# Two rules of a hand-kept instruction order: the second sublayer is left as the table has it, and the later ones move their casts out of both token halves' norms

## The chip, the cores and the metric

The kernel runs on one core of one Trainium2 chip. The metric is device time in microseconds (us) of that core, as the median of several executions. TensorE (PE) does the matrix products and the transposes, VectorE (DVE) and ScalarE (ACT) the elementwise work, GpSimd (POOL) a few small powers and fills, and SyncE (SP) issues all loads and stores. Each engine works through its own list of instructions in the order in which the program puts them there.

## The reference

Two layers, each of three sublayers, six in all: a SwiGLU network, a token mixer and another SwiGLU network. The mixer of the first layer is an indexer-selected sparse attention ("dsa"), that of the second a differential attention ("diff"). Everything is float32: 256 tokens, width 1024, inner width 2752.

```python
for i in range(DEPTH):                       # DEPTH = 2
    mod = cond @ ada_w[i] + ada_b[i]
    sh0, sc0, g0, sh1, sc1, g1, sh2, sc2, g2 = jnp.split(mod, N_MOD, axis=-1)
    h = modulate(rmsnorm(x, pre_norm[i, 0]), sh0, sc0)
    y = swiglu(h, ffn_w_gate[i, 0], ffn_w_up[i, 0], ffn_w_down[i, 0])
    x = x + FFN_HALF * g0[:, None, :] * rmsnorm(y, post_norm[i, 0])
    h = modulate(rmsnorm(x, pre_norm[i, 1]), sh1, sc1)
    y = dsa_mixer(...) if i % 2 == 0 else diff_mixer(...)
    x = x + g1[:, None, :] * rmsnorm(y, post_norm[i, 1])
    h = modulate(rmsnorm(x, pre_norm[i, 2]), sh2, sc2)
    y = swiglu(h, ffn_w_gate[i, 1], ffn_w_up[i, 1], ffn_w_down[i, 1])
    x = x + FFN_HALF * g2[:, None, :] * rmsnorm(y, post_norm[i, 2])
```

## The kernel before

**Two token halves.** The 256 tokens are two halves of 128, t = 0 and t = 1, that go through the six sublayers (n = 0 to 5) one behind the other. In the second FFN part both share a product (`mm_joint`); elsewhere each half has its own matmuls, and the half t = 1 uses a weight block a few blocks after t = 0 did.

**Weights.** Every weight block of 128 rows is loaded in float32 into `raw` (5 buffers), and becomes two tiles: `hi`, a rounded copy, by a CAST on ACT, and `lo`, the rest, by a subtraction on DVE. Each product is three matmuls, activation hi by weight hi, hi by lo, and lo by hi. The pair normally is `whl` (7 buffers in a ring, each free again when t = 1 has used the block). `opens()` marks the first three blocks of a sublayer as early: their pair (`whi`, `wlo`) lies in the pool `big` (11 buffers) instead.

**From one sublayer to the next.** When the last matmul of a half's output is done (`ydown`, `ydsa`, `ydiff`), a chain of small steps leads to the next sublayer's first matmul. The letters are the labels that `link` gives the steps:

- a: ACT squares the two halves of the columns (`junk,ssy`), adds them up (`ssy`, then `rstdy`); POOL takes the power (`rstdy`).
- u: DVE multiplies the output by the gate (`u`); x: DVE adds it to the stream (`x0`, `x1`).
- b: ACT squares and sums the new x (`junk,ss`, `rstd`); POOL takes the power.
- h, r: DVE scales (`h<-x,g`) and modulates (`h<-h,rstd,sh`); t: PE transposes eight blocks (`ps_x`).
- c: ACT casts them to `HT` hi, DVE subtracts to `HT` lo. Then PE starts with `projA` (n = 1), `gate` (n = 2, 3, 5) or `projK` (n = 4).

The vectors `sh`, `g` and `pg` of the modulation are made between all this: POOL clears the tile, DVE accumulates (`sh<-araw`), PE spreads the sum over the partitions (`ps_m`), and ACT or DVE writes the result (`g<-ps_m`).

**What sets the order.** `ORDER`, a table of numbers, gives each engine's whole order; `arranged` then changes it around each sublayer's start, and `keep_order` makes it binding. Before, `arranged` goes over n = 1 to 5. On ACT and DVE it puts the early conversions ahead of the chain of t = 0, and holds weight casts back (`free`) so that only as many as `ROOM` allows stand behind a step a, b, x or r of t = 0. On PE it puts the transposes of t = 0 in among the last matmuls of t = 1's output:

```python
turns = [name for _, p, name in chain if p == "t"]
...
last = order.index(mark["out"][1, n - 1])
order[last - 4:last] = turns[:4] + order[last - 4:last] + turns[4:]
```

All instructions pass through one helper, so the profile gives them all the line L1027; they are told apart by their tiles.

Of the kernel before, what the change touches and what calls it, by code (L numbers as in the profile page):

```python
# [50 lines left out]
def trunk(ctx, tc, x, c, positions, ada_w, ada_b, pre_norm, post_norm, ffn_w_gate, ffn_w_up,  # L51
          ffn_w_down, dsa_w_in, dsa_w_out, diff_w_in, diff_w_out, diff_lambda, diff_subln, out):
    calls = []
    nc = Calls(tc.nc, calls)
# [272 lines left out]
    def ada_items(n, part):  # L327


        l, s = divmod(n, 3)  # L330
# [826 lines left out]
ROOM = {"a": 1, "b": 2, "x": 1, "r": 1}  # L1157


def arranged(orders, mark):  # L1160


    for n in range(1, 6):
        chain = mark["chain"][0, n]
        free = mark["free"] | {name for _, _, name in mark["chain"][1, n]}
        for order in (orders["EngineType.Activation"], orders["EngineType.DVE"]):
            part = {name: p for _, p, name in chain}
            at = [i for i, name in enumerate(order) if name in part]
            left = {p: sum(part.get(name) == p for name in order) for p in set(part.values())}
            new, held, room = [], [], 0  # L1170
            behind = at[-1] + 1
            ahead = [name for name in order[at[0]:behind + 12] if name in mark["early"]]
            for name in ahead:
                order.remove(name)
# [1 line left out]
            at = [i for i, name in enumerate(order) if name in part]
            for name in order[at[0]:at[-1] + 1]:
                if name in free:
                    held.append(name)
                else:  # L1180
                    new.append(name)
                    p = part.get(name)
                    if p:
                        left[p] -= 1
                        room = 0 if left[p] else ROOM.get(p, 0)
                new += held[:room]
                room, held = room - len(held[:room]), held[room:]
            order[at[0]:at[-1] + 1] = new + held
# [30 lines left out]
```

## Time and profile before

| | |
|---|---|
| time before, median of 3 runs | 1061.79 us (1056.61 to 1065.71) |
| the profiled execution's own time | 1061.59 us |
| its span, first to last instruction | 1059.8 us |
| around the span | 1.8 us |
| mean granted TensorE clock | 0.991 |
| busy: PE, DVE, ACT | 1017.6 us, 788.7 us, 522.6 us |

In a timeline a row is one instruction or several equal ones in a run: start in us from the span's start, length in us, engine, line, operation, output<-inputs, shape, count, and in brackets how long the engine stood idle before it and what ended that. PE's matmuls overlap, so a row of many is read by its length over its count. The granted clock is 1.0 at TensorE's 2.4 GHz and 0.5 at 1.2 GHz.

### The profile page before, as it was taken

The numbers are of one execution on the slowest core, as the hardware profiler recorded it, in microseconds if no ns is written. First come the engines' busy times: TensorE is split into PE (matmuls) and PEld (weight loads), VectorE is DVE, ScalarE is ACT, GpSimd is POOL, SyncE is SP. The second block draws the span as 40 slices with busy tenths as digits, with TensorE's granted clock in tenths as the row PEclk, the third lists the DMA queues.
The fourth block names the chain that finished last, engine by engine and source line by source line (L and its number), as shares of the span: only waits on it lengthen the run. The fifth ranks groups of instructions, "written<-read, shape, count | busy, mean of one in ns | idle before, by whom it ended". The sixth has DMA issues, their size and how long they took to land.

```text
span 1059.8 us, 15297 instructions
## 1 busy us (share of the span) xinstructions
PE 1017.6 (96%) x5936; PEld 876.0 (83%) x5936; DVE 788.7 (74%) x1121; ACT 522.6 (49%) x834; POOL 34.9 (3%) x49
## 2 busy tenths in 40 slices
PE   5999999988999999999999999999899899999997
PEld 2679997768777789998888999978777678999875
DVE  4769898887986978876688977857988675765643
ACT  3354434354475744453364544436467665544432
POOL 1000000001000200000010000000100100000000
PEclk9999999998999999999999999999999999999999
DMA  9949889983534477988757879866662533778531
GB/s 309 345 136 316 328 308 375 345 281 140 211 120 150 166 249 261 348 277 300 270 195 267 281 240 334 320 256 221 242 231 85 186 118 122 249 229 266 180 119 40
DMA packets 93732, 249.48 MB, mean 235 GB/s; under 512 B 6084, under 2 KB 24652, under 8 KB 93660
## 3 DMA queue, kind: packets, MB, share of 16 engines
q1 hardware_dynamic: 93660, 248.52, 67.9%
q8 instruction: 46, 0.75, 0.3%
q14 instruction: 26, 0.21, 0.1%
HBM read 247.44 MB, written 1.05 MB: 234 GB/s over the span
## 4 chain that ended last, share of the span: by engine, by line
PE 57%; issue 20%; DVE 5%; ACT 3%; POOL 1%; DMA 0%; DVEq 0%; POOLq 0%; ACTq 0%
PE ydown L1027 15%; PE up L1027 12%; PE gate L1027 11%; PE projQd L1027 2%; PE projQ L1027 2%; PE projA L1027 2%; PE projV L1027 2%; PE projK L1027 2%; PE ydiff L1027 1%; PE dsaS L1027 1%; PE ydsa L1027 1%; PE ps_m L1027 1%; PE diffS L1027 1%; PE dsaO L1027 1%; DVE whl L1027 1%
## 5 line engine op out<-in xcount | busy, mean ns | idle before, releaser
L1027 DVE TENSOR_TENSOR whl<-raw,whl 128x1024 fp32r<-128x1024 f32 (+3 forms) x201 | 228.7, 1151 | 94.9 <-ACT whl L1027 94.0
L1027 ACT CAST whl<-raw 128x1024 fp32r<-128x1024 f32 (+3 forms) x201 | 196.4, 996 | 172.4 <-PE ydown L1027 88.5
L1027 PE MATMUL gate<-HT,wj 128*128 128x256 f32 x1344 | 166.2, 284 | 1.3 <-DVE wj L1027 1.2
L1027 ACT CAST wj<-raw 128x1024 fp32r<-128x1024 f32 x112 | 116.3, 1048 | 103.6 <-PE up L1027 29.0
L1027 PEld LDWEIGHTS gate<-HT,wj 128*128 128x128 f32 x1344 | 163.4, 192 | 2.0 <-DVE wj L1027 1.7
L1027 PE MATMUL up<-HT,wj 128*128 128x256 f32 x1344 | 164.4, 283 | 0.1
L1027 DVE TENSOR_TENSOR wj<-raw,wj 128x1024 fp32r<-128x1024 f32 x112 | 134.8, 1221 | 39.5 <-ACT wj L1027 39.2
L1027 PEld LDWEIGHTS up<-HT,wj 128*128 128x128 f32 x1344 | 162.8, 192 | 0.6 <-ACT wj L1027 0.3
L1027 PE MATMUL ydown<-whl,ffj 128*128 128x512 f32 x672 | 159.3, 393 | 2.3 <-DVE whl L1027 2.3
L1027 PEld LDWEIGHTS ydown<-whl,ffj 128*128 128x128 f32 x672 | 126.0, 189 | 30.4 <-DVE whl L1027 3.1
L1027 PE MATMUL ydown<-whl,ffa 128*128 128x512 f32 (+1 forms) x368 | 90.9, 398 | 1.9 <-ACT whl L1027 1.9
L1027 PEld LDWEIGHTS ydown<-whl,ffa 128*128 128x128 f32 (+1 forms) x368 | 69.0, 191 | 20.2 <-issue 3.6
L1027 PE MATMUL gate<-whl,HT 128*128 128x480 f32 x276 | 71.3, 394 | 0.8 <-DVE whl L1027 0.7
L1027 DVE SCALAR_TENSOR_TENSOR pg<-araw,scond,pg 128x1024 f32<-128x1024 f32 x48 | 61.4, 1280 | 8.2 <-DMA araw<-in_ada_w_dram 7.7
L1027 PE MATMUL up<-whl,HT 128*128 128x480 f32 x288 | 66.0, 381 | 0.0
L1027 PEld LDWEIGHTS gate<-whl,HT 128*128 128x128 f32 x276 | 52.3, 192 | 13.1 <-issue 1.9
L1027 PEld LDWEIGHTS up<-whl,HT 128*128 128x128 f32 x288 | 53.5, 188 | 8.3 <-ACT sg L1027 0.5
L1027 DVE SCALAR_TENSOR_TENSOR g<-araw,scond,g 128x1024 f32<-128x1024 f32 x40 | 51.2, 1280 | 5.4 <-DMA araw<-in_ada_w_dram 4.9
L1027 DVE SCALAR_TENSOR_TENSOR sh<-araw,scond,sh 128x1024 f32<-128x1024 f32 x40 | 51.1, 1278 | 5.3 <-DMA araw<-in_ada_w_dram 5.0
L1027 POOL TENSOR_TENSOR rstdy<-rstdy,mhalf 128x1 f32<-128x1 f32 x12 | 6.6, 549 | 834.2 <-ACT rstdy L1027 834.2
L1027 PE MATMUL projV<-whl,HT 128*128 128x512 f32 x96 | 28.4, 416 | 0.0
L1027 ACT ACTIVATE junk<-x 128x512 f32<-128x512 f32 (+1 forms) x24 | 15.2, 632 | 26.3 <-DVE x L1027 15.2
(223 smaller groups left out, 1179.6 us busy)
## 6 DMA issues: line engine op xcount, KB each, us to landing
araw<-in_ada_w_dram SPq DMA_DIRECT2D x64, 1024.0 KB
raw<-in_ffn_w_down_dram SPq DMA_DIRECT2D x40, 1024.0 KB
raw<-in_ffn_w_gate_dram SPq DMA_DIRECT2D x56, 512.0 KB
raw<-in_ffn_w_up_dram SPq DMA_DIRECT2D x56, 512.0 KB
raw<-in_ffn_w_gate_dram SPq DMA_DIRECT2D x16, 960.0 KB
raw<-in_diff_w_in_dram SPq DMA_DIRECT2D x12, 1024.0 KB
raw<-in_ffn_w_up_dram SPq DMA_DIRECT2D x12, 960.0 KB
fraw<-in_ada_w_dram SPq DMA_DIRECT2D x32, 256.0 KB
```

Of the source, the lines that this page charges most:

```text
L1027: ins = method(*args, **kwargs)
```

## The change

Three things. `opens()` is no longer called ahead of `dsa_w_in`, so the first three blocks of the second sublayer (n = 1) are ordinary `whl` blocks. `arranged` starts at n = 2, so at n = 1 all engines follow the table as it stands. At n = 2 to 5 the holding back of casts (now `tidied`) is done for the chain of t = 1 too, and the writes of `ps_m` that are marked `spread` are put behind the last step b or x of t = 1.

```diff
     add_ffn(0, 0)
-    opens()
     add_matrix(dsa_w_in[0], D, 1024, 712)
...
+def tidied(order, chain, free):
+    part = {name: p for _, p, name in chain}
+    at = [i for i, name in enumerate(order) if name in part]
+    left = {p: sum(part.get(name) == p for name in order) for p in set(part.values())}
+    new, held, room = [], [], 0
+    for name in order[at[0]:at[-1] + 1]:
+        if name in free:
+            held.append(name)
+        else:
+            new.append(name)
+            p = part.get(name)
+            if p:
+                left[p] -= 1
+                room = 0 if left[p] else ROOM.get(p, 0)
+        new += held[:room]
+        room, held = room - len(held[:room]), held[room:]
+    return order[:at[0]] + new + held + order[at[-1] + 1:]
+
 def arranged(orders, mark):
-    for n in range(1, 6):
-        chain = mark["chain"][0, n]
-        free = mark["free"] | {name for _, _, name in mark["chain"][1, n]}
...
+    for n in range(2, 6):
+        chains = [mark["chain"][t, n] for t in range(2)]
+        own = [{name for _, _, name in chain} for chain in chains]
+        for e in ("EngineType.Activation", "EngineType.DVE"):
...
+            ahead = [name for name in order[at[0]:at[-1] + 13] if name in mark["early"]]
+            behind = [name for name in order[at[0]:end] if name in mark["spread"]]
+            order = [name for name in order if name not in set(ahead + behind)]
             order[at[0]:at[0]] = ahead
...
+            order = tidied(order, chains[0], mark["free"] | own[1])
+            order = tidied(order, chains[1], mark["free"])
+            place = max(order.index(name) for _, p, name in chains[1] if p in "bx" and name in order) + 1
+            order[place:place] = behind
```

**The start of the second sublayer (n = 1) on ACT.** `ssy_2009`, `rstdy_2010` and `x0` belong to t = 0; `ydown_1578` is the output of t = 1, and `ssy_2147` (now `ssy_2144`) its sum. Before:

```order
L1027 ACTIVATE rstdy_2010<-ssy_2009 128x1
L1027 CAST whl_2113<-raw_2107 128x712
L1027 ACTIVATE junk_2025,ss_2023<-x0_79 128x512
L1027 ACTIVATE junk_2027,ss_2023<-x0_79 128x513
L1027 ACTIVATE rstd_2024<-ss_2023 128x1
L1027 CAST whl_2192<-raw_2190 128x712
L1027 ACTIVATE junk_2150,ssy_2147<-ydown_1578 128x512
L1027 CAST HT_76<-ps_x_2034 128x512
L1027 CAST HT_76<-ps_x_2044 128x512
L1027 ACTIVATE junk_2153,ssy_2147<-ydown_1578 128x512
```

And now:

```order
L1031 CAST whl_2110<-raw_2105 128x712
L1031 ACTIVATE rstdy_2010<-ssy_2009 128x1
L1031 ACTIVATE junk_2025,ss_2023<-x0_79 128x512
L1031 ACTIVATE junk_2027,ss_2023<-x0_79 128x513
L1031 CAST whl_2189<-raw_2187 128x712
L1031 ACTIVATE rstd_2024<-ss_2023 128x1
L1031 ACTIVATE junk_2147,ssy_2144<-ydown_1578 128x512
L1031 ACTIVATE junk_2150,ssy_2144<-ydown_1578 128x512
L1031 ACTIVATE ssy_2144<-ssy_2144,epsc_83 128x1
L1031 CAST whl_2192<-raw_2187 128x712
L1031 CAST HT_76<-ps_x_2034 128x512
L1031 CAST HT_76<-ps_x_2044 128x512
```

Two casts moved in ahead of `rstdy` and `rstd` of t = 0, and the squares of t = 1 stand ahead of both casts to `HT` and no longer around them. Ahead of these rows both orders have three casts of 712 columns in the same place, to `whi` before and to `whl` now, then the two squares and the sum `ssy` of t = 0.

**The same start on PE.** `ps_x_2034` and `ps_x_2044` are the transposes of t = 0, `projA_2054` its first product. Before:

```order
L1027 MATMUL ydown_1578<-whl_1991,ffj_1575 128x512 x6
L1027 MATMUL ydown_1578<-whl_1994,ffj_1575 128x512
L1027 MATMUL ps_x_2034<-ident_87,h_2031 128x128 x4
L1027 MATMUL ydown_1578<-whl_1994,ffj_1575 128x512 x4
L1027 MATMUL ps_x_2044<-ident_87,h_2041 128x128 x4
L1027 MATMUL ydown_1578<-whl_1994,ffj_1575 128x512
L1027 MATMUL projA_2054<-whi_2063,HT_76 128x384
```

And now:

```order
L1031 MATMUL ydown_1578<-whl_1991,ffj_1575 128x512 x6
L1031 MATMUL ydown_1578<-whl_1994,ffj_1575 128x512 x6
L1031 MATMUL ps_x_2034<-ident_87,h_2031 128x128 x4
L1031 MATMUL ps_x_2044<-ident_87,h_2041 128x128 x4
L1031 MATMUL projA_2054<-whl_2063,HT_76 128x384
```

The last five matmuls of t = 1's output now stand ahead of the transposes of t = 0 and no longer among and behind them.

**The same start on DVE.** `u_2149` (now `u_2146`) is the output of t = 1 times its gate, `x1` its stream. Before:

```order
L1027 SCALAR_TENSOR_TENSOR h_2041<-h_2041,rstd_2024,sh_1400 128x512
L1027 TENSOR_TENSOR u_2149<-ydown_1578,pg_817 128x512
L1027 TENSOR_TENSOR HT_76<-ps_x_2034,HT_76 128x512
L1027 TENSOR_TENSOR HT_76<-ps_x_2044,HT_76 128x512
L1027 TENSOR_TENSOR u_2149<-ydown_1578,pg_817 128x512
L1027 SCALAR_TENSOR_TENSOR x1_81<-u_2149,rstdy_2148,x1_81 128x512 x2
```

And now:

```order
L1031 SCALAR_TENSOR_TENSOR h_2041<-h_2041,rstd_2024,sh_1400 128x512
L1031 TENSOR_TENSOR u_2146<-ydown_1578,pg_817 128x512 x2
L1031 TENSOR_TENSOR HT_76<-ps_x_2034,HT_76 128x512
L1031 TENSOR_TENSOR HT_76<-ps_x_2044,HT_76 128x512
L1031 SCALAR_TENSOR_TENSOR x1_81<-u_2146,rstdy_2145,x1_81 128x512 x2
```

The second `u` moved ahead of the two subtractions to `HT` lo.

**The start of the fourth sublayer (n = 3) on ACT, t = 1.** Before:

```order
L1027 ACTIVATE ssy_4932<-ssy_4932,epsc_83 128x1
L1027 ACTIVATE junk_4938,ssy_4932<-ydown_4455 128x512
L1027 CAST whl_5013<-raw_5011 128x960
L1027 ACTIVATE rstdy_4933<-ssy_4932 128x1
L1027 ACTIVATE junk_4948,ss_4946<-x1_81 128x512
```

And now:

```order
L1031 ACTIVATE ssy_4929<-ssy_4929,epsc_83 128x1
L1031 ACTIVATE junk_4935,ssy_4929<-ydown_4452 128x512
L1031 ACTIVATE rstdy_4930<-ssy_4929 128x1
L1031 CAST whl_5010<-raw_5008 128x960
L1031 ACTIVATE junk_4945,ss_4943<-x1_81 128x512
```

One cast moved from ahead of `rstdy` of t = 1 to behind it. The same single step is taken at n = 2, 4 and 5. Besides, at n = 4 the second of two `g<-ps_m` on DVE moved from behind the steps h and r of t = 1 to ahead of them. POOL's and SP's orders are the same before and after, and so is PE's order from n = 2 on.

## Rows read from the trace of the kernel before

**Rows 1.** The page's part 2, whole program: PE's granted clock in 40 slices of 26.5 us, in tenths of full speed.

```profile
PEclk9999999998999999999999999999999999999999
```

**Rows 2.** Sums by stretch around the start of the second sublayer: stretch in us, its length, busy us and instructions of PE, PEld, DVE, ACT and POOL, then PE's granted clock, DMA share and GB/s.

```profile
238.20:241.50 3.30, 3.29 (x12) 2.80 (x13) 0.62 (x1) 0.00 (x0) 0.00 (x0) 0.50 0.71 279
241.50:244.90 3.40, 1.43 (x7) 0.81 (x5) 0.59 (x1) 2.86 (x8) 0.00 (x0) 1.00 0.00 0
245.00:251.70 6.70, 6.04 (x20) 6.04 (x21) 5.15 (x10) 2.68 (x8) 2.06 (x3) 0.50 0.02 3
251.80:262.30 10.50, 10.26 (x65) 9.84 (x65) 9.88 (x12) 5.56 (x9) 1.91 (x2) 1.00 0.52 164
```

**Rows 3.** PE's timeline at the start of the second sublayer.

```profile
222.19 1.10 PE L1027 MATMUL ps_m<-ahl,onesr 128*128 128x512 f32 x4
...
225.57 9.14 PE L1027 MATMUL ydown<-whl,ffj 128*128 128x512 f32 x39 [1.37 <-DVE whl L1027]
238.21 1.12 PE L1027 MATMUL ps_x<-ident,h 128*128 128x128 f32 x4 [3.50 <-DVE h L1027]
...
243.26 0.59 PE L1027 MATMUL projA<-whi,HT 128*128 128x384 f32 x2 [1.25 <-ACT HT L1027]
...
245.66 1.55 PE L1027 MATMUL projA<-whi,HT 128*128 128x384 f32 x4 [1.48 <-DVE HT L1027]
...
253.06 1.04 PE L1027 MATMUL ps_x<-ident,h 128*128 128x128 f32 x8
254.33 0.59 PE L1027 MATMUL projA<-whi,HT 128*128 128x384 f32 x2 [0.24 <-ACT HT L1027]
```

**Rows 4.** ACT's timeline of the same stretch. The row at 242.63 is the two casts to `HT` of t = 0.

```profile
223.89 2.16 ACT L1027 CAST whi<-raw 128x712 fp32r<-128x712 f32 x3
231.57 0.60 ACT L1027 ACTIVATE junk<-ydown 128x512 f32<-128x512 f32 x1 [5.51 <-PE ydown L1027]
...
232.72 0.29 ACT L1027 ACTIVATE ssy<-ssy,epsc 128x1 f32<-128x1 f32 x1
233.05 0.29 ACT L1027 ACTIVATE rstdy<-ssy 128x1 f32<-128x1 f32 x1
...
236.27 0.29 ACT L1027 ACTIVATE rstd<-ss 128x1 f32<-128x1 f32 x1
...
242.63 1.06 ACT L1027 CAST HT<-ps_x 128x512 fp32r<-128x512 f32 x2
...
244.34 0.80 ACT L1027 CAST whl<-raw 128x712 fp32r<-128x712 f32 x1
245.01 0.32 ACT L1027 ACTIVATE rstdy<-ssy 128x1 f32<-128x1 f32 x1
```

**Rows 5.** DVE's and POOL's timelines of the same stretch.

```profile
234.07 1.40 DVE L1027 SCALAR_TENSOR_TENSOR x<-u,rstdy,x 128x512 f32<-128x512 f32 x2
...
237.41 1.41 DVE L1027 SCALAR_TENSOR_TENSOR h<-h,rstd,sh 128x512 f32<-128x512 f32 x2
...
246.12 0.68 DVE L1027 TENSOR_TENSOR u<-ydown,pg 128x512 f32<-128x512 f32 x1
248.35 1.41 DVE L1027 SCALAR_TENSOR_TENSOR x<-u,rstdy,x 128x512 f32<-128x512 f32 x2 [1.55 <-POOL rstdy L1027]
...
251.69 1.41 DVE L1027 SCALAR_TENSOR_TENSOR h<-h,rstd,sh 128x512 f32<-128x512 f32 x2
...
246.86 0.95 POOL L1027 MEMSET sh<- 128x1024 f32 x1 [9.56 <-DVE u L1027]
247.77 0.55 POOL L1027 TENSOR_TENSOR rstdy<-rstdy,mhalf 128x1 f32<-128x1 f32 x1
```

**Rows 6.** The later sublayers, t = 1: ACT's cast and `rstdy` at n = 3; DVE's steps x at n = 2, 3, 4 and 5, and r at n = 4, with their waits; PE's waits at n = 2, 3, 4 and 5.

```profile
550.30 0.99 ACT L1027 CAST whl<-raw 128x960 fp32r<-128x960 f32 x1
551.19 0.29 ACT L1027 ACTIVATE rstdy<-ssy 128x1 f32<-128x1 f32 x1
...
359.85 1.42 DVE L1027 SCALAR_TENSOR_TENSOR x<-u,rstdy,x 128x512 f32<-128x512 f32 x2 [0.60 <-POOL rstdy L1027]
552.14 1.41 DVE L1027 SCALAR_TENSOR_TENSOR x<-u,rstdy,x 128x512 f32<-128x512 f32 x2 [0.42 <-POOL rstdy L1027]
742.66 1.42 DVE L1027 SCALAR_TENSOR_TENSOR x<-u,rstdy,x 128x512 f32<-128x512 f32 x2 [0.47 <-POOL rstdy L1027]
746.32 1.41 DVE L1027 SCALAR_TENSOR_TENSOR h<-h,rstd,sh 128x512 f32<-128x512 f32 x2 [0.44 <-POOL rstd L1027]
869.71 1.42 DVE L1027 SCALAR_TENSOR_TENSOR x<-u,rstdy,x 128x512 f32<-128x512 f32 x2 [0.42 <-POOL rstdy L1027]
...
362.38 1.57 PE L1027 MATMUL gate<-whl,HT 128*128 128x480 f32 x6 [0.36 <-DVE whl L1027]
364.34 1.29 PE L1027 MATMUL ps_x<-ident,h 128*128 128x128 f32 x8 [0.39 <-DVE h L1027]
554.67 1.58 PE L1027 MATMUL gate<-whl,HT 128*128 128x480 f32 x6 [0.17 <-DVE whl L1027]
556.63 1.29 PE L1027 MATMUL ps_x<-ident,h 128*128 128x128 f32 x8 [0.38 <-DVE h L1027]
747.12 0.66 PE L1027 MATMUL ps_x<-ident,h 128*128 128x128 f32 x4 [2.23 <-DVE h L1027]
874.21 1.29 PE L1027 MATMUL ps_x<-ident,h 128*128 128x128 f32 x8 [0.39 <-DVE h L1027]
```

More of the change, by code (lines that the diff above doesn't have):

```diff
@@ L221, in trunk @@
     W = {}
-    MARK = {"free": set(), "early": set(), "chain": {}, "out": {}}
+    MARK = {"free": set(), "early": set(), "spread": set(), "chain": {}, "out": {}}
     def free(ins):
@@ L230, in early, with spread @@
         MARK["early"].add(ins.ins.name)
+    def spread(ins):
+        MARK["spread"].add(ins.ins.name)
     def link(t, n, part, ins):
@@ L359, in end @@
                 ps = tr_tile("ps_m")
-                nc.tensor.matmul(flat(ps), onesr, hl[:, 0, sl], start=True, stop=False)
-                nc.tensor.matmul(flat(ps), onesr, hl[:, 1, sl], start=False, stop=True)
+                spread(nc.tensor.matmul(flat(ps), onesr, hl[:, 0, sl], start=True, stop=False))
+                spread(nc.tensor.matmul(flat(ps), onesr, hl[:, 1, sl], start=False, stop=True))
                 if part == 0:
-                    nc.scalar.copy(m[:, sl], flat(ps))
+                    ins = nc.scalar.copy(m[:, sl], flat(ps))
                 elif part == 1:
-                    nc.vector.scalar_tensor_tensor(m[:, sl], flat(ps), 1.0, pb[:, sl], op0=OP.add, op1=OP.mult)
+                    ins = nc.vector.scalar_tensor_tensor(m[:, sl], flat(ps), 1.0, pb[:, sl], op0=OP.add, op1=OP.mult)
                 else:
-                    nc.vector.scalar_tensor_tensor(m[:, sl], flat(ps), 1.0 if s == 1 else 0.5, pb[:, sl],
-                                                   op0=OP.mult, op1=OP.mult)
+                    ins = nc.vector.scalar_tensor_tensor(m[:, sl], flat(ps), 1.0 if s == 1 else 0.5, pb[:, sl],
+                                                         op0=OP.mult, op1=OP.mult)
+                spread(ins)
         def item(i):
@@ L1157 @@
 ROOM = {"a": 1, "b": 2, "x": 1, "r": 1}
-def arranged(orders, mark):
-    for n in range(1, 6):
-        chain = mark["chain"][0, n]
-        free = mark["free"] | {name for _, _, name in mark["chain"][1, n]}
[L1166 to L1174, printed above, removed]
-            order[at[0]:at[0]] = ahead
[L1176 to L1188, printed above, removed]
@@ new lines, in arranged @@
+def arranged(orders, mark):
+    for n in range(2, 6):
+        chains = [mark["chain"][t, n] for t in range(2)]
+        own = [{name for _, _, name in chain} for chain in chains]
+        for e in ("EngineType.Activation", "EngineType.DVE"):
+            order = orders[e]
+            at = [i for i, name in enumerate(order) if name in own[0]]
+            end = max(i for i, name in enumerate(order) if name in own[1])
+            ahead = [name for name in order[at[0]:at[-1] + 13] if name in mark["early"]]
+            behind = [name for name in order[at[0]:end] if name in mark["spread"]]
+            order = [name for name in order if name not in set(ahead + behind)]
+            order[at[0]:at[0]] = ahead
+            order = tidied(order, chains[0], mark["free"] | own[1])
+            order = tidied(order, chains[1], mark["free"])
+            place = max(order.index(name) for _, p, name in chains[1] if p in "bx" and name in order) + 1
+            order[place:place] = behind
+            orders[e] = order
@@ L1190, in arranged @@
         order = orders["EngineType.PE"]
-        turns = [name for _, p, name in chain if p == "t"]
+        turns = [name for _, p, name in chains[0] if p == "t"]
         for name in turns:
```

## The prediction

> **What bounds the kernel now.** PE is busy for 1017.6 of 1059.8 us, so time can be won where PE waits, or where it works at its lower clock. I read the clock by slices first: one slice away from the very start and end stands below the rest, the tenth, from 238 us on [rows 1]. The sums by stretch then show two stretches at half clock in it, 238.2 to 241.5 and 245.0 to 251.7 [rows 2], and PE's timeline shows why PE had stopped: 3.50 us for the first transposes of t = 0, 1.25 for `HT` hi, 1.48 for `HT` lo, 0.24 for `HT` hi of t = 1 [rows 3]. That is the start of the second sublayer (n = 1), just where the change takes the rearrangement away. Together 6.5 us of waiting, and at half clock 20 matmuls in 6.04 us, 0.302 each, against 65 instructions in 10.26 us, 0.158 each, at full clock [rows 2]: those 20 alone lose 2.9 us. At the later sublayers PE waits 0.4 to 0.8 us (2.2 at n = 4) for t = 1 [rows 6].
>
> **n = 1, the three first conversions** stay in their places on ACT, but now need buffers of the ring of seven. They ran from 223.89 on [rows 4]; the three blocks whose buffers they get were used up by t = 1 ahead of the `ps_m` at 222.19 [rows 3]. So they wait for nothing, by a margin of 1.5 us or so, and I take 0. Were the cover gone, each block would cost six matmuls of 0.234 (39 in 9.14 us [rows 3]), 1.4 us, and the squares of t = 0 queue behind them on ACT. The pool `big` is left six tiles emptier, which only removes waits.
>
> **n = 1, the chain of t = 0** gets two casts of 712 columns put into it, ahead of `rstdy` and ahead of `rstd`. One holds the next step up by 0.67 (244.34 to 245.01); `rstdy` used to start 0.33 after `ssy`, part of which the cast fills [rows 4]. Step x stood waiting for the power of `rstdy` (234.07 [rows 5]), and step r for that of `rstd`. I take 0.55 each, 1.1 in all (bounds 1.0 and 1.35). Step r goes from 237.41 to 238.5 [rows 5], the first transpose from 238.21 to 239.3 [rows 3].
>
> **n = 1, PE meanwhile.** It goes on with the five matmuls of t = 1 that used to stand among and behind the transposes: 234.71 plus 5 x 0.234 is 235.9. Its wait is then 239.3 - 235.9 = 3.4 us, as long as before (3.50), so I let the clock fall to half again. What has changed is what comes behind it. The outputs of t = 1 are complete at 235.9, not at 242.0, so its squares (1.44 us from 231.57 to the end of `ssy` for t = 0 [rows 4]) and the cast behind them fit on ACT between `rstd` (237.7) and 239.9. Four transposes at half clock take 1.1 us [rows 3]; ACT casts from 240.4, and PE starts `projA` at 241.0 (was 243.26). Both `u` run from 239.9 to 241.2 at 0.68 each [rows 5], the first `HT` lo, of the same size, is there at 241.9, and PE's first four matmuls last until 241.0 + 4 x 0.302 = 242.2. So the wait of 1.48 goes too: 32 matmuls without a stop, where before the remaining 28 began at 245.66 and ended at 253.06 [rows 3].
>
> **How long the clock stays low** decides when they end. The first half-clock stretch ended 3.3 us after PE had begun again (238.2 to 241.5), the second 6.1 us after (245.66 to 251.8) [rows 2, 3]. I take the longer, since the new stretch begins with transposes and a short stop: full clock from 239.3 + 6.1 = 245.4. Then 14 matmuls at 0.302 and 18 at 0.158 end at 248.1. With the shorter, five at half and 27 at full end at 246.8; with half clock throughout, at 241.0 + 32 x 0.302 = 250.7.
>
> **n = 1, is t = 1 ready then?** Before, the second `u` stood behind `HT` lo on DVE, POOL's clearing of `sh` waited for it (246.86, 0.95 long), and `rstdy` of t = 1 queued behind that on POOL, which gave x at 248.35 [rows 5]. Now both `u` are done at 241.2, the clearing ends at 242.2, the power at 242.8, x starts there, r 3.34 later (251.69 - 248.35 [rows 5]) at 246.1, and its first half is done at 246.9. PE, at 248.1, comes later and decides; it resumes 1.27 after its transposes begin (253.06 to 254.33 [rows 3]), at 249.4. **Gain at n = 1: 254.33 - 249.4 = 4.9 us**, bounds 1.9 (all at half, the transposes 0.5 longer) and 6.1 (t = 1's chain decides). Behind this point the casts of four more blocks wait for t = 1 to use blocks 0 to 3. DVE, busy 9.88 of 10.50 us there [rows 2], makes the other half of the same blocks later than ACT does, which hides it; uncovered it would cost six matmuls, 0.95 us, for a block. The loads are hidden: the DMA share is 0.00 and 0.02 from 241.5 to 251.7 [rows 2].
>
> **n = 2 to 5.** Ahead of `rstdy` of t = 1 a cast of 0.89 us goes away (550.30 to 551.19). DVE stood idle before step x for 0.60, 0.42, 0.47 and 0.42 us because of it [rows 6]; ahead of that come the `u`, so no more than this is won. At n = 4 one `g<-ps_m`, as large as a `u` (0.68), now stands ahead of h and r, where only 0.44 were idle (746.32), so 0.24 goes back and 0.23 is left [rows 6]. 0.60 + 0.42 + 0.23 + 0.42 = 1.7. PE's waits there are as large: 0.36 + 0.39, 0.17 + 0.38, 2.23 and 0.39 [rows 6]. The cast goes behind `rstdy`, where ACT waits for x anyway. **Gain: 1.7 us**, bounds 0 and 1.9.
>
> **Sum.** 4.9 + 1.7 = 6.6 us. The profiled execution's own time is 1061.59, 0.2 below the median of the three runs; 1061.6 - 6.6 = **1055.0 us**.
>
> **Rivals.** (1) The clock stays at half through all 32 matmuls: 1.9 + 1.7 gives 1058.0. For it: the eight transposes no longer have matmuls among them, and the second stretch was the longer one although PE worked through most of it [rows 2]. Against it: the first stretch had eight transposes in it, beside four matmuls, and ended at full clock.
> The Trainium skill, page "TensorE: Matmul & The Clock Gate", section "Part 4: PE-mode transpose", says that transposes do not count as PE work for the clock in the way matmuls do. By that rule the stretch would go this way, to the 1058.0 of this rival; the trace, with its mixed stretch, does not decide it.
> (2) The clock comes back as fast as after 238.2, and t = 1's chain decides: 6.1 + 1.7 gives 1053.8. For it: 32 matmuls follow without the stops that came before the second stretch.
> (3) The gain of n = 1 is eaten further on, since DVE is busy for 94% of the time from 251.8 to 262.3 [rows 2] and both halves' attention follows: only 1.7 stays, 1059.9. Against it: DVE's list is the same there and starts as much earlier as PE does, and nothing that comes from outside is late.
> (4) Slower: the clock stays at half beyond the resumption too. The 8.0 us of work from 254.33 to 262.3 would take 0.302/0.158 times as long, 7.3 more: 1061.6 - 3.6 + 7.3 = 1065.3. It turns to a loss when more than some 7.5 us behind the resumption run at half. For it: the wait of 3.4 us that sends the clock down is still there. Against it: from 251.8 on full clock was held in spite of the 0.24 wait.
>
> **How the numbers follow.** Forecast 0.50, rival (1) 0.20, (2) 0.15, (3) 0.10, (4) 0.05. The three runs of before lie 9 us apart, so a median may be off by 3 in either direction: the range goes from 1050 to 1060.5, which takes in rivals (1) to (3) and leaves out (4). A change of under 1%, 10.6 us, is about what a measurement of this kernel can not tell from none. Faster by more needs under 1051.2, rival (2) with a favourable spread or the clock never falling: 0.16. Slower by more needs rival (4) with an unfavourable one: 0.03. Within 1%: 0.81.
>
> **What would show it.** PE's timeline: the first transposes of t = 0 a good 1 us later, all eight together after a wait of 3.4 us, `projA` starting at about 241 with no wait for `HT` lo, and t = 1's transposes at 247 to 250. POOL's clearing of `sh` at 241, and x of t = 1 right behind it. The sums by stretch: one half-clock stretch in place of two. At n = 2, 3 and 5, DVE without a wait before x. It is wrong if the first three casts wait on ACT, if a second half-clock stretch follows, or if new waits of PE stand between 250 and 340 us.

## The result: 1055.0 us, and the profile after

The changed kernel takes 1054.97 us (median of 14 runs, 1050.64 to 1059.80), the kernel before 1061.26 beside it (14 runs, 1056.61 to 1065.91): a ratio of 0.9941, 95% interval 0.9921 to 0.9960, so 6.3 us less (4.2 to 8.4). The forecast was 1055.0, and "within 1%".

The profiled execution took 1051.05, span 1049.2, 10.6 us under the span of before; it is one of the fastest of the 14, with a mean granted clock of 0.997. First PE at the start of the second sublayer, to be read beside [rows 3] (the helper's line is now L1031):

```profile
222.94 10.27 PE L1031 MATMUL ydown<-whl,ffj 128*128 128x512 f32 x44 [1.37 <-DVE whl L1031]
236.59 1.31 PE L1031 MATMUL ps_x<-ident,h 128*128 128x128 f32 x8 [3.39 <-DVE h L1031]
237.92 6.98 PE L1031 MATMUL projA<-whl,HT 128*128 128x384 f32 x32
244.75 1.04 PE L1031 MATMUL ps_x<-ident,h 128*128 128x128 f32 x8
246.02 3.21 PE L1031 MATMUL projA<-whl,HT 128*128 128x384 f32 x18 [0.24 <-ACT HT L1031]
```

Of the three waits of 3.50, 1.25 and 1.48 us one of 3.39 is left, and `projA` runs through. ACT, DVE and POOL there, beside [rows 4, 5]:

```profile
228.94 0.60 ACT L1031 ACTIVATE junk<-ydown 128x512 f32<-128x512 f32 x1 [5.46 <-PE ydown L1031]
...
234.67 0.29 ACT L1031 ACTIVATE rstd<-ss 128x1 f32<-128x1 f32 x1
234.87 0.57 ACT L1031 ACTIVATE junk<-ydown 128x512 f32<-128x512 f32 x1
...
237.28 1.25 ACT L1031 CAST HT<-ps_x 128x512 fp32r<-128x512 f32 x2 [0.32 <-PE ps_x L1031]
```
```profile
231.91 1.42 DVE L1031 SCALAR_TENSOR_TENSOR x<-u,rstdy,x 128x512 f32<-128x512 f32 x2 [0.39 <-POOL rstdy L1031]
...
234.06 1.29 DVE L1031 TENSOR_TENSOR h<-x,g 128x512 f32<-128x512 f32 x2
235.78 1.41 DVE L1031 SCALAR_TENSOR_TENSOR h<-h,rstd,sh 128x512 f32<-128x512 f32 x2 [0.44 <-POOL rstd L1031]
...
243.30 1.41 DVE L1031 SCALAR_TENSOR_TENSOR h<-h,rstd,sh 128x512 f32<-128x512 f32 x2
```
```profile
235.04 0.71 POOL L1031 TENSOR_TENSOR rstd<-rstd,mhalf 128x1 f32<-128x1 f32 x1 [3.16 <-ACT rstd L1031]
238.46 0.95 POOL L1031 MEMSET sh<- 128x1024 f32 x1 [2.71 <-DVE u L1031]
```

The squares of t = 1 stand at 234.87, right behind `rstd` and before the casts to `HT`. The sums by stretch, columns as in [rows 2], show one half-clock stretch of 3.4 us, 237.85 to 241.27, in place of the two at this place before:

```profile
234.40:237.85 3.45, 1.25 (x8) 0.84 (x8) 3.01 (x6) 3.13 (x9) 0.71 (x1) 1.00 0.76 223
237.85:241.27 3.42, 3.40 (x12) 3.32 (x12) 3.06 (x5) 2.01 (x5) 1.46 (x2) 0.50 0.22 87
241.30:244.70 3.40, 3.40 (x22) 3.40 (x22) 3.40 (x7) 1.12 (x5) 1.54 (x2) 1.00 0.00 0
```

PE's transposes of t = 1 at n = 2 to 5, beside [rows 6]:

```profile
355.32 0.96 PE L1031 MATMUL ps_x<-ident,h 128*128 128x128 f32 x5 [0.33 <-DVE h L1031]
547.05 1.29 PE L1031 MATMUL ps_x<-ident,h 128*128 128x128 f32 x8 [0.30 <-DVE h L1031]
736.97 0.66 PE L1031 MATMUL ps_x<-ident,h 128*128 128x128 f32 x4 [1.73 <-DVE h L1031]
863.66 1.29 PE L1031 MATMUL ps_x<-ident,h 128*128 128x128 f32 x8 [0.33 <-DVE h L1031]
```

DVE's step x of t = 1 at n = 2, beside its wait of 0.60 in [rows 6]; at n = 3, 4 and 5 it starts without a wait as well:

```profile
350.84 1.41 DVE L1031 SCALAR_TENSOR_TENSOR x<-u,rstdy,x 128x512 f32<-128x512 f32 x2
```

**Where the time went, in the two traces.** At the first squares of t = 0 the new kernel is 2.63 us ahead (228.94 against 231.57 [rows 4]), which the change can't have made: the engines' orders up to there are the same. The trace of before has two more stretches at half clock, 19.7 to 23.1 and 176.7 to 180.1 us, that this one lacks; the lead goes from -0.1 to 1.1 us around the first and from 1.0 to 2.6 around the second. In the slices of [rows 1] they don't show, since 3.4 us of half clock leave a slice of 26.5 us above 0.9. One or both are in two other traces of the changed kernel, so this part is chance. From the first squares to the resumption the new kernel needs 17.08 us instead of 22.76 (246.02 and 254.33 [rows 3]): **5.7 us at n = 1**. The lead is then 8.31, and at the transposes of t = 1 at n = 2, 3, 4, 5 it is 9.02, 9.58, 10.15 and 10.55: **2.2 us at the later sublayers**, 0.71, 0.56, 0.57 and 0.40.

### The profile page after: what moved, and what is told of

It reads as the page before. It is cut to its first block, busy times and chain, and to the rows that moved or that the text cites. A ratio compares the mean times of both kernels' runs of the same rounds, so it can differ in the third digit from the quotient of the medians.

```text
span 1049.2 us, 15301 instructions
## 1 busy us (share of the span) xinstructions
PE 1010.5 (96%) x5936; PEld 871.1 (83%) x5936; DVE 788.5 (75%) x1121; ACT 523.7 (50%) x834; POOL 35.1 (3%) x49
## 4 chain that ended last, share of the span: by engine, by line
PE 63%; issue 20%; DVE 8%; ACT 4%; DMA 3%; POOL 1%; SPq 0%; DVEq 0%; POOLq 0%; ACTq 0%
PE ydown L1031 16%; PE gate L1031 13%; PE up L1031 12%; PE projQd L1031 2%; PE projQ L1031 2%; DVE wj L1031 2%; PE projV L1031 2%; PE projA L1031 2%; PE projK L1031 2%; PE ydiff L1031 1%; DMA raw<-in_ffn_w_gate_dram 1%; PE ps_mod L1031 1%; PE dsaS L1031 1%; PE ydsa L1031 1%; PE diffS L1031 1%
## 5 line engine op out<-in xcount | busy, mean ns | idle before, releaser
L1031 DVE TENSOR_TENSOR whl<-raw,whl 128x1024 fp32r<-128x1024 f32 (+3 forms) x204 | 231.2, 1148 | 96.1 <-ACT whl L1031 95.1
L1031 ACT CAST whl<-raw 128x1024 fp32r<-128x1024 f32 (+3 forms) x204 | 198.6, 993 | 170.9 <-PE ydown L1031 88.5
L1031 ACT CAST wj<-raw 128x1024 fp32r<-128x1024 f32 x112 | 116.6, 1049 | 106.6 <-PE up L1031 30.4
L1031 PE MATMUL gate<-HT,wj 128*128 128x256 f32 x1344 | 166.2, 284 | 1.7 <-DVE wj L1031 1.7
L1031 DVE TENSOR_TENSOR wj<-raw,wj 128x1024 fp32r<-128x1024 f32 x112 | 135.0, 1221 | 42.5 <-ACT wj L1031 42.2
L1031 PEld LDWEIGHTS gate<-HT,wj 128*128 128x128 f32 x1344 | 163.4, 192 | 2.4 <-DVE wj L1031 2.1
L1031 PE MATMUL up<-HT,wj 128*128 128x256 f32 x1344 | 164.4, 283 | 0.0
L1031 PEld LDWEIGHTS up<-HT,wj 128*128 128x128 f32 x1344 | 162.8, 192 | 0.4
L1031 PE MATMUL ydown<-whl,ffj 128*128 128x512 f32 x672 | 157.8, 391 | 2.2 <-DVE whl L1031 2.2
L1031 PEld LDWEIGHTS ydown<-whl,ffj 128*128 128x128 f32 x672 | 125.5, 188 | 30.3 <-DVE whl L1031 3.1
L1031 PE MATMUL ydown<-whl,ffa 128*128 128x512 f32 (+1 forms) x368 | 89.3, 393 | 1.9 <-ACT whl L1031 1.9
L1031 PEld LDWEIGHTS ydown<-whl,ffa 128*128 128x128 f32 (+1 forms) x368 | 67.9, 188 | 19.7 <-issue 3.6
L1031 PE MATMUL gate<-whl,HT 128*128 128x480 f32 x276 | 69.1, 387 | 0.1
L1031 DVE SCALAR_TENSOR_TENSOR pg<-araw,scond,pg 128x1024 f32<-128x1024 f32 x48 | 61.4, 1280 | 6.7 <-DMA araw<-in_ada_w_dram 6.1
L1031 PE MATMUL up<-whl,HT 128*128 128x480 f32 x288 | 65.9, 380 | 0.0
L1031 PEld LDWEIGHTS gate<-whl,HT 128*128 128x128 f32 x276 | 51.4, 188 | 11.2 <-issue 1.9
L1031 PEld LDWEIGHTS up<-whl,HT 128*128 128x128 f32 x288 | 53.5, 188 | 8.3 <-ACT sg L1031 0.5
L1031 DVE SCALAR_TENSOR_TENSOR g<-araw,scond,g 128x1024 f32<-128x1024 f32 x40 | 51.2, 1280 | 5.1 <-DMA araw<-in_ada_w_dram 4.7
L1031 DVE SCALAR_TENSOR_TENSOR sh<-araw,scond,sh 128x1024 f32<-128x1024 f32 x40 | 51.2, 1279 | 3.7 <-DMA araw<-in_ada_w_dram 3.3
L1031 POOL TENSOR_TENSOR rstdy<-rstdy,mhalf 128x1 f32<-128x1 f32 x12 | 6.6, 549 | 830.4 <-ACT rstdy L1031 830.4
L1031 PE MATMUL projV<-whl,HT 128*128 128x512 f32 x96 | 28.4, 416 | 0.0
L1031 ACT CAST HT<-ps_x 128x512 fp32r<-128x512 f32 (+1 forms) x28 | 14.5, 526 | 26.5 <-PE ps_x L1031 26.1
```

The costliest lines, as they stand in the source:

```text
L1031: ins = method(*args, **kwargs)
```

## The experiments

All were timed beside the kernel before on the same chip, in three lots (e1 to e4, e5 to e8, e9 to e12), each on another chip. The changed kernel itself ran in the last two as well, as a control:

| | median, us | kernel before, us | ratio, 95% interval |
|---|---|---|---|
| e1_second_alone | 1056.90 | 1064.22 | 0.9922, 0.9897 to 0.9948 |
| e2_later_alone | 1059.87 | 1064.22 | 0.9965, 0.9943 to 0.9987 |
| e3_early_pairs | 1055.66 | 1064.22 | 0.9911, 0.9886 to 0.9936 |
| e4_turns_moved | 1061.66 | 1064.22 | 0.9968, 0.9949 to 0.9988 |
| e5_casts_out | 1058.10 | 1066.38 | 0.9921, 0.9886 to 0.9957 |
| e6_fill | 1054.69 | 1066.38 | 0.9898, 0.9873 to 0.9924 |
| e7_casts_out_fill | 1055.00 | 1066.38 | 0.9896, 0.9868 to 0.9924 |
| e8_after_again | 1055.48 | 1066.38 | 0.9902, 0.9877 to 0.9927 |
| e9_no_room | 1069.34 | 1064.24 | 1.0048, 1.0031 to 1.0065 |
| e10_second_too | 1072.15 | 1064.24 | 1.0074, 1.0050 to 1.0099 |
| e11_all_fill | 1071.83 | 1064.24 | 1.0078, 1.0051 to 1.0104 |
| e12_after_third | 1055.07 | 1064.24 | 0.9915, 0.9893 to 0.9937 |

The changed kernel stood at 1055.0, 1055.5 and 1055.1; the kernel before at 1061.3, 1064.2, 1066.4 and 1064.2. So the gain is 6.3 us in the first timing and 9 to 11 in the others. The mean granted clock over the runs of before was 0.9885, 0.9874 and 0.9884 in the three lots, that of the changed kernel 0.9940 and 0.9930 in the last two, so part of the gain is fewer stretches at half clock. Between executions with the same mean clock, 4 to 6 us are left: at 0.989, 1059.0 to 1059.8 (three of the changed kernel) against 1062.5 to 1066.6 (13 of before, median 1063.6), and at 0.992, 1055.2 to 1056.7 (three) against 1059.9 to 1062.9 (four). Some of the better clock is the change's own doing, the stretch that is gone at n = 1. Why before stood lower in the first timing stays open.

In what follows, "after the first square" counts from ACT's first square of t = 0 at n = 1 in the same trace, which leaves out what happened before.

**The change's two places, one at a time.**

```diff
     add_ffn(0, 0)
-    opens()
...
-    for n in range(1, 6):
+    for n in range(2, 6):
```

> The kernel before with the change at the second sublayer alone: no early conversions there, nothing moved there; n = 2 to 5 keep the old rules (casts held back for t = 0 only). Theory: the second sublayer is where most of the gain is, so about 4.9 us (by the sum on record) to 5.7 us (by the two traces) off the kernel before, a ratio of 0.9946 to 0.9954, and t = 1's PE at n = 2 to 5 waits for the h steps as before (0.39, 0.38, 2.2, 0.39 us). Rival: what n = 1 wins is eaten further on and the later sublayers make the difference; then within 1 us of the kernel before.

Measured: 7.3 us below the kernel before by the medians, 8.3 by the ratio, more than expected, though the interval (0.9897 to 0.9948) reaches the expected 0.9946. PE resumes 17.11 after the first square, as in the changed kernel (17.08), and t = 1's transposes at n = 3 and 4 wait 0.39 and 2.23 us again; at n = 2 and 5 they wait 0.93 and 0.91, which is taken up below, with the power for `rstd`.

The other half of the change, `tidied` and `spread` as in the diff, on n = 2 to 5, with n = 1 and `opens()` as before:

> The change at n = 2 to 5 alone: the second sublayer keeps its early conversions and its rearrangement as in the kernel before. Theory: 1.7 us (the sum on record) to 2.2 us (the shifts between the two traces) off the kernel before, a ratio of 0.9979 to 0.9984, and two half-clock stretches at the second sublayer as before. Rival: the later casts behind the power delay blocks that t = 0 or t = 1 needs, and 0 or a loss of up to 1 us is seen. Together with the run of the second sublayer alone the two gains should add to the 6.3 us of the whole change, if they are independent.

Measured: 4.35 us below by the medians, 3.7 by the ratio, whose interval takes in the expected 0.998. With e1's 7.3 it makes 11.7 us, as against 8.6 for e3 beside them, which has both; the intervals are too wide to tell this from plain adding up. The start of the second sublayer in this trace:

```profile
237.62 0.66 PE L1032 MATMUL ps_x<-ident,h 128*128 128x128 f32 x4 [3.51 <-DVE h L1032]
...
241.14 0.59 PE L1032 MATMUL projA<-whi,HT 128*128 128x384 f32 x2 [1.25 <-ACT HT L1032]
...
243.54 1.55 PE L1032 MATMUL projA<-whi,HT 128*128 128x384 f32 x4 [1.48 <-DVE HT L1032]
...
252.25 0.59 PE L1032 MATMUL projA<-whi,HT 128*128 128x384 f32 x2 [0.24 <-ACT HT L1032]
```

The three waits of [rows 3] to a hundredth, but one half-clock stretch (242.9 to 249.7), not two, and PE resumes 21.27 after the first square (230.98), not 22.76. So the old arrangement costs 4.2 us more than the new one here, and 5.7 in the execution of before: 1.5 us of the 5.7 hung on where the clock fell.

**Which part of the second sublayer's rearrangement cost.** Early conversions put back (`opens()` in the changed kernel):

> The changed kernel with one part undone: the first three blocks of the second sublayer are early again, with their pairs in the pool of eleven, while every engine follows the table there. Theory: the early conversions cost nothing and bring nothing by themselves, since the first casts waited for nothing in both traces: within 0.5 us of the changed kernel, some 6.3 us below the kernel before. Rival: the pairs in the pool of eleven hold up later tiles there or free ring buffers that the casts behind HT wait for (1.17, 0.52 and 0.90 us of ACT waiting after the change); then 1 us or more off the changed kernel in either direction.

Measured: 1055.66, 0.2 to 0.7 above the changed kernel's medians, none of which is of this lot; PE resumes 17.17 after the first square. The early conversions by themselves are worth nothing that shows.

Only the transposes put back among t = 1's matmuls:

```diff
+    order = orders["EngineType.PE"]
+    turns = [name for _, p, name in mark["chain"][0, 1] if p == "t"]
...
+    order[last - 4:last] = turns[:4] + order[last - 4:last] + turns[4:]
```

> The changed kernel with one part undone: only PE's transposes of t = 0 at the second sublayer stand again in among the last matmuls of t = 1's output, four ahead of the last four matmuls and four behind; ACT and DVE follow the table. Theory: the transposes' place is what delayed t = 1's output (242.0 against 235.9), and so its squares and its u, and what split PE's start into waits; it costs 3 to 5 us of the changed kernel's gain, so 1 to 3 us below the kernel before, with two half-clock stretches or one long one. Rival: the loss came from ACT's and DVE's order (squares around the HT casts, u behind HT lo); then within 1 us of the changed kernel.

Measured: 6.0 us above e3 beside it, and by the resumption 22.10 after the first square, 5.0 more than the changed kernel. PE and ACT:

```profile
238.74 0.66 PE L1031 MATMUL ps_x<-ident,h 128*128 128x128 f32 x4 [4.53 <-DVE h L1031]
...
241.51 0.78 PE L1031 MATMUL ydown<-whl,ffj 128*128 128x512 f32 x1
244.99 7.09 PE L1031 MATMUL projA<-whl,HT 128*128 128x384 f32 x32 [2.70 <-ACT HT L1031]
```
```profile
242.32 0.60 ACT L1031 ACTIVATE junk<-ydown 128x512 f32<-128x512 f32 x1 [5.22 <-PE ydown L1031]
...
243.67 0.78 ACT L1031 CAST whl<-raw 128x712 fp32r<-128x712 f32 x1
244.34 1.08 ACT L1031 CAST HT<-ps_x 128x512 fp32r<-128x512 f32 x2
```

The transposes come no earlier for it (7.66 after the first square, as in the changed kernel: they wait for h), but the outputs of t = 1 are complete only behind them. ACT stands 5.22 us before t = 1's squares, and the casts to `HT`, which stand behind the squares, come after that: 2.70 us of waiting at `projA`, and half clock from 239.4 to 242.8 and 246.2 to 249.6. So PE's order by itself, with ACT and DVE in the table's order, is enough to lose 5.0 us. The reverse, PE in the table's order and ACT and DVE as before, was not run: what their old order costs by itself is not shown. Nor is this the loss of before step by step: there the casts to `HT` stood ahead of the second square and PE waited 1.25 for them, and then 1.48 for `HT` lo [rows 3].

**The cost of leaving the chain of t = 0 with its two casts, and the clock.**

```diff
+    for e in ("EngineType.Activation", "EngineType.DVE"):
+        orders[e] = tidied(orders[e], mark["chain"][0, 1], mark["free"])
```

> The changed kernel with one thing added: at the second sublayer the two weight casts that stand ahead of rstdy and of rstd in the chain of t = 0 go behind these steps; PE's order and the early conversions stay as in the changed kernel. Theory: they are the price of leaving that sublayer alone, 0.55 us each, so PE's wait for the first transposes falls from 3.39 to about 2.3 us and 1.1 us more is gained (up to 2.8 if the shorter wait keeps the clock up): a ratio to the changed kernel of about 0.999 (0.9973 to 0.999). Rival: the casts come too late for projA's blocks and PE waits there instead, or t = 1's chain ends last after all; then no gain.

Measured: 1058.1, 2.6 us above the changed kernel in the same lot, its interval still overlapping. The seven executions fall apart by their mean clock: three at 0.993 and 0.994 took 1053.7 to 1054.7, one at 0.991 took 1058.1, and three at 0.986 to 0.988 took 1060.4 to 1062.7. The changed kernel's six beside them all had 0.994 and took 1054.6 to 1055.9, so at that clock e5 is about 1 us faster, as expected, but three executions don't settle it. The trace is of one of these last (0.988). The wait fell to 2.91, not 2.3. DVE's and POOL's rows:

```profile
235.29 1.29 DVE L1031 TENSOR_TENSOR h<-x,g 128x512 f32<-128x512 f32 x2
237.03 1.41 DVE L1031 SCALAR_TENSOR_TENSOR h<-h,rstd,sh 128x512 f32<-128x512 f32 x2 [0.44 <-POOL rstd L1031]
```
```profile
235.74 1.25 POOL L1031 TENSOR_TENSOR rstd<-rstd,mhalf 128x1 f32<-128x1 f32 x1 [2.67 <-ACT rstd L1031]
```

x starts 2.51 after the first square instead of 2.97, so the first cast's half microsecond is won. The second is not: the power starts at once behind `rstd`, but it ends 0.41 us behind DVE's steps h, after 1.25 us, and r starts 3.87 after x as with the cast in place. In the kernel before the same power, asked for 0.43 after h had begun (here 0.45), took 0.66. And the clock was low for 6.8 us (237.0 to 243.8), which takes back the rest: PE resumes 17.46 after the first square. Another stretch at half clock lay at 325.7 to 336.0 us, in the attention, where PE had no wait; none of the other traces has it, and it is not explained.

Filling the wait instead, so that PE never stops for long:

```diff
+        if (t, n) == (1, 0):
+            ps = flat(s_tile("fill"))
+            for _ in range(FILL):
+                fills.append(tc.nc.tensor.matmul(ps, onesr, HT[:, 1, 0, 0:4, :], start=True, stop=True))
```

> The changed kernel with 13 matmuls of 128x512 added to PE (about 0.234 us each, 3.0 us), whose result nobody reads, in its wait of 3.39 us ahead of the first transposes of t = 0 at the second sublayer. Their output bank lies in the ring that the attention uses later. Theory: it is the wait that makes the clock fall there; without it the 32 projA matmuls run at full clock throughout, 5.3 us and not 6.98, so 1.7 us less wherever the changed kernel has a half-clock stretch at this place, and t = 1's chain then is what PE waits for, which gives back some of it: 0.5 to 1.7 us below the changed kernel. Rival: the clock falls there by chance, as it does in stretches elsewhere, or transposes alone send it down; then no gain.

Measured: 0.8 us below the control, which the runs can't tell from none.

```profile
232.42 3.19 PE L620 MATMUL fill<-HT,onesr 128*128 128x512 f32 x13
235.97 1.32 PE L1040 MATMUL ps_x<-ident,h 128*128 128x128 f32 x8 [0.36 <-DVE h L1040]
237.31 0.92 PE L1040 MATMUL projA<-whl,HT 128*128 128x384 f32 x4
238.43 4.85 PE L1040 MATMUL projA<-whl,HT 128*128 128x384 f32 x28 [0.21 <-DVE HT L1040]
244.10 1.29 PE L1040 MATMUL ps_x<-ident,h 128*128 128x128 f32 x8 [0.82 <-DVE h L1040]
```

The clock stays at full level (1.00 from 237.3 to 243.2), and in e7's trace too it does not fall; behind a wait of 3.39 or 3.40 us it fell within 2 us in all six traces that have one at this place. So it was the wait that sent it down there, though not always at once: in e2, behind 3.51 us, it fell only after the next wait. `projA` is through in 5.97 us, but PE then waits 0.82 for h of t = 1 and resumes 17.10 after the first square. t = 1's chain ends when PE at half clock would be done as well: here the clock was worth nothing. But in this trace the power of t = 1's `rstd` took 1.20 us, in the changed kernel's 0.59, so that r started 1.23 behind the power's start and not 0.70. An estimate from these two traces is that filling the wait is worth up to 0.5 us where the power is quick.

> Both together: the two casts out of the chain of t = 0 at the second sublayer, and 9 matmuls (2.1 us) whose result nobody reads in the wait of about 2.3 us that is left. Theory: the two gains add as far as t = 1's chain allows, 1.5 to 2.8 us below the changed kernel (1052 to 1053.5 where that has 1055). Rival: PE then waits for t = 1's transposes by what the clock gives, and no more than the 1.1 us of the casts is seen.

Measured: 1055.00, 0.5 below the control, no gain that shows, though in its trace PE resumes 16.61 after the first square, 0.5 earlier. The power of t = 0 and that of t = 1 took 1.25 and 1.19 us there.

**The power for rstd.** By then the traces held the same power at the same place with two lengths. At n = 3, t = 1, it is asked for 0.24 us after h has begun, and takes 0.85 in one execution of the changed kernel and 1.45 in another; PE's wait for h is 0.30 in the first and 0.87 in the second. The second, e8:

```profile
548.74 1.45 POOL L1031 TENSOR_TENSOR rstd<-rstd,mhalf 128x1 f32<-128x1 f32 x1 [1.53 <-DMA sh<-in_ada_b_dram]
```
```profile
551.13 1.07 PE L1031 MATMUL ps_x<-ident,h 128*128 128x128 f32 x6 [0.87 <-DVE h L1031]
```

That also explains the 0.93 and 0.91 of e1, where the power took 1.46 at both places. The next run moves h away from the power by another order:

```diff
-ROOM = {"a": 1, "b": 2, "x": 1, "r": 1}
+ROOM = {"a": 1, "b": 2, "x": 0, "r": 1}
```

> The changed kernel with the room behind a step x set from 1 to 0: at n = 2 to 5 the one lo subtraction (0.9 us) that DVE makes between x and h of t = 1 goes behind r. Theory: POOL's power for rstd is held up while DVE multiplies x by g, both in SBUF: in the traces so far it takes 0.55 us with DVE idle, 0.85 to 0.98 where it gets in between the two steps h, 1.45 where it does not, and r starts up to 1.49 us after it is asked for. With h right behind x, both steps h are nearly done when the power is asked for: it takes 0.55 to 0.7, r starts 0.6 to 0.75 after, 0.3 to 0.9 us earlier at each of four sublayers, and PE's waits there (0.33 to 0.87 us, 1.74 at n = 4) shrink by as much: 1 to 2.5 us below the changed kernel, and less spread from run to run. Rival: the subtraction is missed by PE, which then waits for whl ahead of t = 1's transposes; then no gain, or up to 1 us lost.

Measured: 14.3 us above the control of its lot (e12). At n = 2, POOL, DVE and PE:

```profile
355.43 0.55 POOL L1031 TENSOR_TENSOR rstd<-rstd,mhalf 128x1 f32<-128x1 f32 x1 [1.53 <-ACT rstd L1031]
```
```profile
354.12 1.29 DVE L1031 TENSOR_TENSOR h<-x,g 128x512 f32<-128x512 f32 x2
356.02 1.42 DVE L1031 SCALAR_TENSOR_TENSOR h<-h,rstd,sh 128x512 f32<-128x512 f32 x2 [0.60 <-POOL rstd L1031]
357.35 1.15 DVE L1031 TENSOR_TENSOR whl<-raw,whl 128x960 fp32r<-128x960 f32 x1
```
```profile
358.55 2.62 PE L1031 MATMUL gate<-whl,HT 128*128 128x480 f32 x6 [2.90 <-DVE whl L1031]
360.97 1.63 PE L1031 MATMUL ps_x<-ident,h 128*128 128x128 f32 x8
...
365.08 0.70 PE L1031 MATMUL gate<-whl,HT 128*128 128x480 f32 x2 [1.25 <-DVE whl L1031]
```

On the power the theory holds: 0.55 us at n = 2, 3 and 5 for t = 1, here and in e10 and e11, no scatter, r 0.58 after it is asked for. On the time the rival wins, at more than its price. The subtraction that stood between x and h (1.15 us here, not 0.9) was due: PE asks for that block at 355.65 (358.55 less 2.90), and t = 1's transposes, ready or not, stand behind it in PE's list. From the transposes of t = 0 to those of t = 1 it now takes 13.22, 13.96 and 14.24 us at n = 2, 3 and 5 against 9.55, 10.71 and 10.70 in e12, 10.5 in all, and the waits behind them (1.25, 0.83, 1.39) make most of the rest. Part of it is the clock: behind the waits of 2.90, 2.88 and 2.88 us it fell to half for 3.4 us each time (358.8 to 362.2 at n = 2), which in e12 it did at none of the three.

> The same, and at the second sublayer too the casts and subtractions are held back for both halves (PE's order and the early conversions as in the changed kernel). Theory: the cast ahead of rstdy, the subtraction ahead of h and the late power go from t = 0's chain: the first transposes come 6.5 us after t = 0's first square (7.66 in the changed kernel, 7.18 where only the casts were taken out), t = 1's chain is as much earlier, and PE, at half clock for a while, decides: 1 us below the run with no room, 2 to 3 below the changed kernel. Rival: the blocks that were converted in between come late for projA, and PE waits for whl; then no gain over the run with no room.

(The rule of e9 and the loop of e5 over both halves' chains.) Measured: 2.8 above e9 by the medians, with intervals that overlap. The first transposes come 6.46 us after the first square, as expected, and the power takes 0.55. But PE waits for blocks:

```profile
235.48 1.32 PE L1031 MATMUL ps_x<-ident,h 128*128 128x128 f32 x8 [2.19 <-DVE h L1031]
...
245.15 2.15 PE L1031 MATMUL projA<-whl,HT 128*128 128x384 f32 x6 [2.54 <-DVE whl L1031]
...
250.95 3.38 PE L1031 MATMUL projA<-whl,HT 128*128 128x384 f32 x19 [1.21 <-DVE whl L1031]
```

The block in question is needed at 242.6 and its subtraction now begins at 244.20, behind r of t = 1.

> The last kernel with 8 matmuls of 128x512 (1.9 us) added in PE's wait ahead of the first transposes of t = 0 at the second sublayer; nobody reads their result. Theory: with full clock there and t = 1's chain no longer held up, PE resumes after t = 1's transposes about 15 us after t = 0's first square, against 17.1 in the changed kernel: 3 to 4.5 us below that in all. Rival: as with the two earlier fills, t = 1's chain decides, and the clock is worth nothing: within 0.5 us of the kernel without the fill.

Measured: within 0.3 us of e10. PE waits for the same blocks (2.62 and 1.29 us) and resumes 19.51 after the first square: the rival.

The controls:

> The changed kernel itself once more, beside these three and the two-part runs, since the kernel before stood 3 us higher on the last chip. Theory: the ratio to the kernel before is 0.9941 as in the first timing, at most 0.003 off either way, about 6 us. If it is 0.991 as in the run with early pairs, that kernel equals the changed one also in the median.

> The changed kernel itself, on the same chip as these three, for the comparison with them: a ratio to the kernel before of 0.990 to 0.994, and the power for rstd taking 0.85 or 1.45 us at n = 2, 3 and 5 by chance, as in its two profiles so far.

Measured: 0.9902 and 0.9915, lower than the first 0.9941, with intervals that overlap; 0.9902 is a little further off than the 0.003 expected. PE resumes 17.29 and 17.09 after the first square. The power at n = 2, 3, 5 took 0.85, 1.45, 1.45 in e8 and 0.85 three times in e12.

None of these kernels is measurably faster than the changed one.

## Why the prediction was right

**n = 1, first conversions: right.** They end at 223.5 with no wait of ACT; e3 shows that their place is indifferent.

**n = 1, the chain of t = 0: right in size, half right in cause.** 1.1 us was predicted; the first transposes come 7.65 us after the first square against 6.64, 1.0 more. The cast ahead of `rstdy` costs 0.47 of it. The other 0.53 was put on the cast ahead of `rstd`, which does put the power off; but e5 and e7, without that cast, kept the delay, because the power, asked for 0.5 us earlier against DVE's h, then took 1.25 us. The prediction had no term for that.

**PE meanwhile: right.** A wait of 3.39 (predicted 3.4, clock down), all outputs of t = 1 ahead of it, its squares before the casts to `HT`, no wait for `HT` lo. e4 shows that undoing this one reordering on PE loses nearly the whole gain of n = 1 again.

**The clock: mis-sized.** Half clock was taken for 6.1 us from PE's restart on. It began 1.3 us after the restart and ended 4.7 us after it, so nearly all of the eight transposes still ran at full clock and `projA` began 0.45 us earlier than predicted (8.98 after the first square; 241.0 - 231.57 = 9.43). One stretch of 3.4 us, begun 0.6 to 1.8 us after the restart, is what the three traces of the changed kernel, e1, e3 and e9 (the same at n = 1) show; e5 shows 6.8, begun before the restart. Rival (1), half clock for all 32 matmuls because transposes led them, did not come in any of them. The Trainium skill's rule behind it (page "TensorE: Matmul & The Clock Gate", section "Part 4: PE-mode transpose", that transposes don't count as PE work in the same way) would, as the prediction applied it, have given 1058.0; these traces don't bear that out, and whether the rule holds by itself no run here shows.

**Is t = 1 ready: nearly level.** Its transposes were put at 248.1 - 231.57 = 16.5 after the first square, with its chain ready at 15.3. They came at 15.8, with the first half of h done at 15.1 and PE the later of the two, as predicted but by less. In e6, at full clock throughout, they came at 15.8 too, since h then was late (the power took 1.20; its first half was done at 15.65). So the bound that the prediction gave to rival (2), t = 1's chain, is within half a microsecond or so of where the changed kernel stands.

**Gain at n = 1:** 4.9 predicted, 5.7 in the pair of profiles, 4.2 against e2's trace of the old arrangement.

**n = 2 to 5: 1.7 predicted, 2.2 measured,** 0.71, 0.56, 0.57, 0.40 for 0.60, 0.42, 0.23, 0.42. The step that failed within this sum is n = 4: the moved `g<-ps_m` was to give 0.24 back. With it the steps h begin 0.6 us later relative to the power, which then ends while the second of them runs and no longer behind it (it is 0.98 us long before and after), and the idle 0.44 ahead of r vanishes: r starts 1.09 instead of 1.01 behind the power's start, 0.08 lost and not 0.24.

**Sum:** 7.9 us in the two profiles, 6.3 (4.2 to 8.4) in the first timing, 9 to 11 in the later ones, against 6.6. That the median came out at the forecast 1055.0 is luck in part: the two terms were off by 0.5 to 0.8 us, and the forecast started from 1061.6, while the kernel before stood at 1064.2 to 1066.4 in the later lots. What held in every timing is a gain of about this size or more. Rival (3), that the gain is eaten further on, is excluded by the growing lead of the two traces; rival (4) needed a second half-clock stretch behind the resumption, and none came there; PE's longest wait from 250 to 340 us is 0.58, as before.

## What to carry to other kernels

Work that is pulled forward on the busiest engine for one half pushes the other half's last matmul back, and with it everything that waits for that half's output: look at both chains before moving transposes into a tail. Before a step is moved behind a chain, find the matmul that needs it and the time at which it does; here 1.15 us of conversion put behind the steps h and r cost 4 to 5 us at each of three sublayers, the lower clock included, since PE keeps its order. A wait that sends the clock down is worth filling, as e6 and e7 show, only where PE, and not another chain, comes last behind it.

## What the runs showed of the hardware that was not expected

POOL's power on 128 values took 0.55 us beside DVE's u (whose input `ydown` is in PSUM) or with DVE idle, but 0.59 to 1.46 beside h<-x,g, whose inputs are both in SBUF. Where the two overlapped by more than a few hundredths of a microsecond, in every trace, it ended 0.4 us after the end of either the first or the second of DVE's two steps h, and from the same start both were seen (0.66 and 1.25, 0.85 and 1.45); a slip costs PE 0.5 to 0.6 us where it waits for h (0.30 and 0.87 at n = 3), and next to nothing where PE comes last (n = 1 in e12: 0.07). The Trainium skill, page "SBUF — State Buffer", section "SBUF: two separate sides", says that VectorE and GpSimd share a pair of ports, held as an exclusive lock by a VectorE instruction with two SBUF inputs; by that rule a GpSimd instruction that reads SBUF, as this power does, waits for the whole of the other, and the lengths agree. Why one start has two outcomes is open.

The granted clock also fell where PE had no wait of note: at 325.7 to 336.0 us in e5, with PE busy all the time. And the same wait had either outcome: ahead of t = 1's transposes at n = 4 PE waited 1.73 or 1.74 us in all three traces of the changed kernel, and the clock fell behind it in one (740.4 to 743.8 in e12). Such stretches come and go between executions of one kernel, and with them most of the scatter of its times: the three executions of the changed kernel in the first timing with a mean clock of 0.997 took 1050.6 to 1051.4, the two with 0.989 took 1059.0 and 1059.8.
